# A second tile for ScalarE's tap products in a 31-tap convolution

## The chip, the cores and the metric

The kernel runs on one core of one Trainium2 chip. The metric is device time in microseconds (us) for one execution. Five instruction streams of the core matter here: TensorE (PE, with its weight loads PEld), VectorE (DVE), ScalarE (ACT), GpSimd (POOL) and SyncE (SP, which issues most DMAs). Each of them takes its instructions strictly in the order in which they stand in its stream.

## The reference

One decoder layer over 2048 tokens of width 1024: a modulated RMSNorm, one input projection whose columns feed three mixers (a gated recurrence "HGRN", a sparse attention with an indexer and top-k, and a convolution module), an output projection, and an MLP of width 4096. The change concerns the convolution module only:

```python
def conv_module(u, cv_w, cv_b, ln_w, ln_b):
    a, b = jnp.split(u, 2, axis=-1)
    h = a * jax.nn.sigmoid(b)
    h = lax.conv_general_dilated(h, cv_w[:, None, :], ...,   # causal, one filter of 31 taps
        feature_group_count=CV_WIDTH) + cv_b                 # for each of 256 channels
    ... LayerNorm over channels, then silu
```

## The kernel before

The sequence is worked in four blocks of 512 tokens. For each block `in_block` runs the input projection as a row of units: each unit is one column block of the weights, multiplied with the block's activations on PE (`mm_T`, line 427, 24 products of 128x128 by 128x512 each, or `n_part`, line 1293, for the units whose result is wanted by token). The first block splits its weights into a high and a low part on the way (ACT line 320, then POOL line 321); later blocks reload what was split. Each unit's result is evicted from PSUM by ACT and DVE (`ev_...` functions).

Everything else is written as generators in queues ("fast" for HGRN, "conv" for the convolution, "idx", "tk" and "at" for the attention, "ada" for modulation vectors) which `step` and `half` advance between the units. That sets the order in which instructions are emitted. A scheduler then orders each engine's stream by its own simulated timeline of the whole program, so a change in the waits of one step can move others.

The convolution of a block lies with channels on partitions and tokens along the row, in two halves of 128 channels (`m` = 0, 1). The units `cb` and `ca` make the gated input: `ev_cb` writes the sigmoid into a tile with the tag `csg0` or `csg1` (line 573), `ev_ca` multiplies it into `hc` (line 579), after which the `csg` tile is free until the half's sum `cacc` is written to the same tag (line 605). `conv_gen` then works a half's 31 taps. Tap 0 and the even taps are a chain on DVE that accumulates in PSUM (`cx`, lines 588 and 600). The odd taps are products on ACT (tap 1 into `cside`, line 594, the other 14 into `ctap`, line 597), which POOL adds to `cside` one after the other (line 598). Line 605 on DVE joins both. `CB = 1`, so there is one `ctap` tile: ACT's next product has to wait until POOL has read the last one. `cx` and `cside` have one buffer as well, so the second half starts after line 605 of the first.

Two other chains share these engines in the same stretch of time. HGRN (`hgrn_gen`) goes through seven levels, each with small products on PE (lines 684, 709, 717) and updates of `q` and `k` on DVE (lines 674, 675, after lines 681 and 692). The top-k search runs passes on DVE (line 931) and ends in a branch (lines 945 to 948, with the exact search that is rarely taken behind it).

Of the kernel before, what the change touches and what calls it, by code (L numbers as in the profile page):

```python
# [8 lines left out]
F32 = mybir.dt.float32  # L9
# [11 lines left out]
P = 128  # L21
D = 1024
L = 2048
TB = 512
# [38 lines left out]
CT = 2  # L63
# [4 lines left out]
CB = 1  # L68
# [10 lines left out]
def trunk(ctx, tc, x, c, ada_w, ada_b, norm_mix_w, norm_mlp_w, w_in, hg_lb_logits,  # L79
# [22 lines left out]
    def nm(s):  # L102
        uid[0] += 1
        return f"{s}_{uid[0]}"

    def dma(o, i):
        return nc.sync.dma_start(o, i)
# [10 lines left out]
    def ps_cx():  # L118
        return px["p"].tile([P, 512], F32, tag="cx", bufs=1, name=nm("cx"))
# [9 lines left out]
    def ps_xp(i):  # L129
        return {'0': ps_ax, '1': ps_mm, '2': ps_at, '3': ps_po}[XP[i]]()  # L130
# [58 lines left out]
    def col(key, i=0, n=1):  # L189
        return cols[:, offs[key] + i:offs[key] + i + n]  # L190
# [62 lines left out]
    def rpow(dst, src, w, scale):  # L253
        G.tensor_scalar(dst, src, scale, EPS, op0=OP.mult, op1=OP.add)
        G.tensor_tensor(dst, dst, nhalf.to_broadcast([P, w]), OP.pow)
# [189 lines left out]
    hp = S1.enter_context(tc.tile_pool(name="hgrn", bufs=1))  # L445
# [9 lines left out]
    def st(tag, bufs, w=TB, dt=F32, shape=None):  # L455
        return hp.tile(shape or [P, w], dt, tag=tag, bufs=bufs, name=nm(tag))
# [126 lines left out]
    def conv_gen(b):  # L583
        accs = []
        for m in range(2):
            hc = conv[m]
            acc = ps_cx()
            V.tensor_scalar(acc, hc[:, 0:TB], cvc[:, m, 0:1], col("cvb", m), op0=OP.mult, op1=OP.add)
            side = None
            for w in range(1, TAPS):  # L590
                if w % CT == 1:
                    if side is None:
                        side = hp.tile([P, TB], F32, tag="cside", bufs=1, name=nm("cside"))
                        A.mul(side, hc[:, w:w + TB], cvc[:, m, w:w + 1])
                    else:
                        tap = hp.tile([P, TB], F32, tag="ctap", bufs=CB, name=nm("ctap"))
                        A.mul(tap, hc[:, w:w + TB], cvc[:, m, w:w + 1])  # L597
                        G.tensor_tensor(side, side, tap, OP.add)  # L598
                else:
                    V.scalar_tensor_tensor(acc, hc[:, w:w + TB], cvc[:, m, w:w + 1], acc,  # L600
                                           op0=OP.mult, op1=OP.add)
                if w % 3 == 0:
                    yield 1300
            total = hp.tile([P, TB], F32, tag=f"csg{m}", bufs=1, name=nm("cacc"))
            V.tensor_tensor(total, acc, side, OP.add)
            accs.append(total)
        yield 1200
        tot = st("cside", 1)
        G.tensor_tensor(tot, accs[0], accs[1], OP.add)
        pm = ps_xp(4)  # L610
        T.matmul(pm, o256.to_broadcast([P, P]), tot, start=True, stop=True)
        for m in range(2):
            V.tensor_tensor(accs[m], accs[m], pm, OP.subtract)
        sqs = []
        for m in range(2):
            sq = st("cu", 2)
            A.activation(sq, accs[m], AF.Square)
            sqs.append(sq)
        G.tensor_tensor(sqs[0], sqs[0], sqs[1], OP.add)
        yield 1500  # L620
        pv = ps_xp(5)
        for t in range(4):
            T.matmul(pv[:, t:t + 1], sqs[0][:, t * P:(t + 1) * P], ones[:, 0:1], start=True, stop=True)
        rc = hp.tile([P, 4], F32, tag="crs", bufs=1, name=nm("crs"))
        V.tensor_copy(rc, pv[:, :4])
        rpow(rc, rc, 4, 1.0 / 256.0)
        yield 1500
        rs = ps_xp(6)
        for t in range(4):
            T.matmul(rs[:, t * P:(t + 1) * P], rc[:, t:t + 1].to_broadcast([P, P]), ident, start=True, stop=True)  # L630
        for m in range(2):
            V.scalar_tensor_tensor(accs[m], accs[m], col("lnw", m), rs, op0=OP.mult, op1=OP.mult)
            sg = st("cu", 2)
            A.activation(sg, accs[m], AF.Sigmoid, bias=col("lnb", m))
            o = st("cu", 2)
            V.scalar_tensor_tensor(o, accs[m], col("lnb", m), sg, op0=OP.add, op1=OP.mult)
            dma(mx_d[b][6 + m], o)
        yield 3000
# [491 lines left out]
    def in_block(b, xts, nxt):  # L1130
        act = first_units(xts) if b == 0 else to_act(xts, a1, sh1, half if TM else None)
        for u, (pieces, ev, m) in enumerate(in_units):
# [38 lines left out]
            if ev is ev_ca and m == 1:  # L1171
                queues["conv"].append(conv_gen(b))
# [94 lines left out]
    for b in range(NB):  # L1267
        for what, g, f in mlp_order(b):
            if what == "out":
                specs += kept_specs("out", out_specs())  # L1270
            elif what == "strassen":
                for kind, g_, i in strassen_order(b):
                    if kind == "m1":
                        specs += kept_specs((kind, g_, i), None)
                    else:
                        w = PRODUCTS[i][1]
# [403 lines left out]
```

## Time and profile before

| | us |
|---|---|
| median of 3 runs | 2960.59 (2958.34 to 2962.74) |
| the profiled execution | 2951.88 |
| its span (first to last instruction) | 2950.1 |
| PE busy | 2794.7 (95%) |
| DVE busy | 1681.9 (57%) |
| ACT busy | 1297.8 (44%) |
| POOL busy | 1239.4 (42%) |

The busy times are sums over the span; stages differ. The convolution's instructions lie between 118 and 946 us, one group for each of the four blocks. Idle time of an engine costs only where another engine, in the end PE, waits for it.

### The profile page before, as it was taken

The numbers are of one execution on the slowest core, as the hardware profiler recorded it, in microseconds if no ns is written. First come the engines' busy times: TensorE is split into PE (matmuls) and PEld (weight loads), VectorE is DVE, ScalarE is ACT, GpSimd is POOL, SyncE is SP. The second block draws the span as 40 slices with busy tenths as digits, with TensorE's granted clock in tenths as the row PEclk, the third lists the DMA queues.
The fourth block names the chain that finished last, engine by engine and source line by source line (L and its number), as shares of the span: only waits on it lengthen the run. The fifth ranks groups of instructions, "written<-read, shape, count | busy, mean of one in ns | idle before, by whom it ended". The sixth has DMA issues, their size and how long they took to land. (4 is left out here: it accounts for less than half of the span.)

```text
span 2950.1 us, 42864 instructions
## 1 busy us (share of the span) xinstructions
PE 2794.7 (95%) x14116; PEld 2313.0 (78%) x14116; DVE 1681.9 (57%) x3450; ACT 1297.8 (44%) x2706; POOL 1239.4 (42%) x1163
## 2 busy tenths in 40 slices
PE   6999989899999989999998999999999999999997
PEld 5888878778788867788786888877788888777776
DVE  7684586966536354847849637385853221254455
ACT  4445464545324235556545544444553333243333
POOL 7573251225214255567656322224432223335444
PEclk9999999899999999999999999999999999999999
DMA  8977666566655567899978867677686767686666
GB/s 284 291 250 238 207 209 216 187 202 196 212 188 170 189 227 247 268 288 307 297 244 271 283 206 225 202 217 253 229 285 207 233 204 232 212 276 222 227 228 208
DMA packets 428075, 688.62 MB, mean 233 GB/s; under 512 B 43383, under 2 KB 171452, under 8 KB 427836
## 3 DMA queue, kind: packets, MB, share of 16 engines
q1 hardware_dynamic: 427680, 685.67, 72.2%
q8 instruction: 113, 1.85, 0.3%
q14 instruction: 126, 1.03, 0.1%
q10 hardware_dynamic: 156, 0.07, 0.0%
HBM read 532.74 MB, written 152.84 MB: 232 GB/s over the span
## 5 line engine op out<-in xcount | busy, mean ns | idle before, releaser
L427 PE MATMUL mm<-ah,wk 128*128 128x512 f32 x1920 | 518.9, 402 | 5.2 <-DVE adrow L780 2.5
L427 PEld LDWEIGHTS mm<-ah,wk 128*128 128x128 f32 x1920 | 359.6, 192 | 80.1 <-DVE adrow L780 3.1
L321 POOL TENSOR_TENSOR wlo<-wraw,whi 128x512 fp32r<-128x512 f32 x210 | 287.7, 1390 | 204.2 <-ACT whi L320 142.5
L1011 POOL TENSOR_TENSOR pT<-L,pT 128x512 fp32r<-128x512 f32 (+3 forms) x160 | 194.1, 1214 | 309.8 <-ACT pT L1010 194.0
L829 DVE SCALAR_TENSOR_TENSOR s<-r,iw_s,s 128x512 f32<-128x512 f32 (+3 forms) x266 | 242.3, 911 | 113.4 <-ACT r L824 104.3
L427 PE MATMUL mm<-al,wk 128*128 128x512 f32 x960 | 262.9, 396 | 0.0
L981 DVE CUSTOM_DVE_ANT_0 L<-at,bias 128x512 f32<-128x512 f32 (+3 forms) x152 | 93.4, 618 | 223.8 <-PE at L979 183.8
L427 PEld LDWEIGHTS mm<-al,wk 128*128 128x128 f32 x960 | 179.9, 190 | 36.2
L1317 PE MATMUL mm<-wk,hh 128*128 128x512 f32 x640 | 199.5, 400 | 2.6 <-DVE acc L1570 2.0
L824 ACT ACTIVATE r<-ix 128x512 f32<-128x512 f32 (+3 forms) x256 | 133.5, 554 | 154.3 <-PE ix L822 107.2
L273 POOL TENSOR_TENSOR hl<-hr,hh 128x512 fp32r<-128x512 f32 x96 | 128.0, 1334 | 172.6 <-ACT hh L265 149.1
L598 POOL TENSOR_TENSOR cside<-cside,ctap 128x512 f32<-128x512 f32 x112 | 149.5, 1335 | 110.4 <-ACT ctap L597 102.6
L320 ACT CAST whi<-wraw 128x512 fp32r<-128x512 f32 x210 | 121.5, 619 | 152.8 <-DMA wraw<-in_mlp_w_dram 37.3
L427 PE MATMUL ax<-ah,wk 128*128 128x512 f32 x720 | 186.4, 393 | 1.1 <-DMA wk<-wk_d 1.1
L931 DVE TENSOR_SCALAR_CACHE_REDUCE cum<-s,ssm 128x384 bf16<-128x384 f32 (+13 forms) x112 | 165.4, 1477 | 7.9 <-POOL s L833 5.7
L427 PEld LDWEIGHTS ax<-ah,wk 128*128 128x128 f32 x720 | 134.4, 188 | 31.1 <-ACT hc L1451 1.5
L1009 ACT COPY L<-at 128x512 f32<-128x512 f32 (+3 forms) x160 | 82.8, 521 | 171.1 <-PE at L1001 169.3
L1477 PE MATMUL mm<-wk,hc 128*128 128x512 f32 x588 | 148.1, 397 | 3.9 <-DVE acc L1485 3.7
L995 ACT ACTIVATE L<-L,nmx 128x512 f32<-128x512 f32 (+3 forms) x160 | 103.7, 650 | 100.4 <-DVE nmx L990 100.0
L1317 PEld LDWEIGHTS mm<-wk,hh 128*128 128x128 f32 x640 | 118.1, 189 | 28.7 <-DVE acc L1570 2.4
L1477 PEld LDWEIGHTS mm<-wk,hc 128*128 128x128 f32 x588 | 109.6, 188 | 33.8 <-DVE acc L1485 7.5
L1317 PE MATMUL ax<-wk,hh 128*128 128x512 f32 x384 | 123.4, 400 | 0.6 <-DVE acc L1570 0.3
(368 smaller groups left out, 6338.5 us busy)
## 6 DMA issues: line engine op xcount, KB each, us to landing
wk<-wk_d SPq DMA_DIRECT2D x776, 256.0 KB, 4.4
wk<-wk_d SPq DMA_DIRECT2D x196, 512.0 KB, 5.1
wk_d<-whi SPq DMA_DIRECT2D x210, 256.0 KB, 3.5
wk_d<-wlo SPq DMA_DIRECT2D x210, 256.0 KB, 5.5
wraw<-in_mlp_w_dram SPq DMA_DIRECT2D x68, 512.0 KB, 5.8
kc<-sk_d SPq DMA_DIRECT2D x112, 256.0 KB, 3.0
vc<-v_d SPq DMA_DIRECT2D x112, 256.0 KB, 4.3
adw<-in_ada_w_dram SPq DMA_DIRECT2D x128, 128.0 KB, 3.4
```

What stands on the lines that cost most here:

```text
L273: e.tensor_tensor(lo[:, i:j], src[:, i:j], hi[:, i:j].bitcast(F32), OP.subtract)
L320: A.copy(hi, src)
L321: G.tensor_tensor(lo, src, hi.bitcast(F32), OP.subtract)
L427: T.matmul(ps, ww[k], aa[k], start=(n == 0 and k0 == 0), stop=(n == len(order) - 1 and k1 == NK))
L598: G.tensor_tensor(side, side, tap, OP.add)
L824: A.activation(r[:, :w], ps[:, :w], AF.Relu, scale=32.0 ** -0.5)
L829: V.scalar_tensor_tensor(s[:, c0:c0 + w], r[:, :w], iw, s[:, c0:c0 + w], op0=OP.mult, op1=OP.add)
L931: V.tensor_scalar(dump, s, t, -AIM - i * STEP, op0=OP.is_ge, op1=OP.add, accum_out=d)
L995: A.activation(lt[:, :w], lt[:, :w], AF.Exp, bias=nmx, accum_out=sm[:, cb:cb + 1])
L1011: G.tensor_tensor(pT[:, :nt, 1], lv, pT[:, :nt, 0].bitcast(F32), OP.subtract)
L1317: T.matmul(ps, aa[f][:, tok * P:(tok + 1) * P], ww[i], start=(first and n == 0), stop=(last and n == 5))
L1477: T.matmul(bank[t], aa[:, k, t * P:(t + 1) * P], ww[k], start=(i in (0, 2, 4) and n == 0), stop=(n == 5), skip_group_check=True)
```

## The change

The 14 products that follow the first one now alternate between two tiles: the old `ctap` tile, and the tile of the tag `csg1`, which held the second half's gate. Both have one buffer. Tap 3 goes to `csg1`, tap 5 to `ctap`, and so on.

```diff
                     else:
-                        tap = hp.tile([P, TB], F32, tag="ctap", bufs=CB, name=nm("ctap"))
+                        tap = hp.tile([P, TB], F32, tag=("ctap", "csg1")[w // CT % 2], bufs=1, name=nm("ctap"))
                         A.mul(tap, hc[:, w:w + TB], cvc[:, m, w:w + 1])
                         G.tensor_tensor(side, side, tap, OP.add)
```

Number and kind of the instructions stay the same on every engine. Their order changes, since the scheduler places them anew: within the four convolution stretches on all engines, and at a few places of the MLP. Three places follow.

POOL, first block, the start of the second half (`cside_1956` is this half's sum, `wlo` the low parts of weights). Before:

```order
L598 TENSOR_TENSOR cside_1956<-cside_1956,ctap_1959 128x512
L598 TENSOR_TENSOR cside_1956<-cside_1956,ctap_2026 128x512
L321 TENSOR_TENSOR wlo_2043<-wraw_1962,whi_2042 128x512
L321 TENSOR_TENSOR wlo_2047<-wraw_1962,whi_2046 128x512
L598 TENSOR_TENSOR cside_1956<-cside_1956,ctap_2030 128x512
L598 TENSOR_TENSOR cside_1956<-cside_1956,ctap_2034 128x512
L321 TENSOR_TENSOR wlo_2136<-wraw_2040,whi_2135 128x512
L321 TENSOR_TENSOR wlo_2140<-wraw_2040,whi_2139 128x512
```

and in the changed kernel:

```order
L598 TENSOR_TENSOR cside_1956<-cside_1956,ctap_1959 128x512
L948 UNCONDITIONAL_BRANCH
L598 TENSOR_TENSOR cside_1956<-cside_1956,ctap_2026 128x512
L598 TENSOR_TENSOR cside_1956<-cside_1956,ctap_2030 128x512
L254 TENSOR_SCALAR hrs_1436<-hrs_1436 128x4
L321 TENSOR_TENSOR wlo_1965<-wraw_1883,whi_1964 128x512
L255 TENSOR_TENSOR hrs_1436<-hrs_1436,nhalf 128x4
L598 TENSOR_TENSOR cside_1956<-cside_1956,ctap_2034 128x512
L321 TENSOR_TENSOR wlo_1969<-wraw_1883,whi_1968 128x512
L598 TENSOR_TENSOR cside_1956<-cside_1956,ctap_2116 128x512
L321 TENSOR_TENSOR wlo_2043<-wraw_1962,whi_2042 128x512
L321 TENSOR_TENSOR wlo_2047<-wraw_1962,whi_2046 128x512
```

Five adds of the second half stand before `wlo_2043` where there were two, and the half begins a unit earlier.

DVE, first block, the joining add of the first half (`cacc_1952`), with the eviction `slo` of projection units around it. Before, it stands behind the top-k branch, among the first steps after it:

```order
L900 MATCH_REPLACE s_747<-top_2038,s_747 128x384
L932 TENSOR_SCALAR ssm_2227<-ssm_2227 128x1
L939 TENSOR_SCALAR ssm_2227<-ssm_2227 128x1
L605 TENSOR_TENSOR cacc_1952<-cx_1350,cside_1352 128x512
L902 TENSOR_SCALAR bias_995<-s_747 128x384
L940 TENSOR_SCALAR ssm_2227<-ssm_2227 128x1
L543 SCALAR_TENSOR_TENSOR slo_1928<-mm_1893,shi_1927 128x512
L588 TENSOR_SCALAR cx_1954<-hc_1334,cvc,cols 128x512
```

and in the changed kernel, ahead of the branch (which follows `L946`):

```order
L742 SCALAR_TENSOR_TENSOR sa_1398<-sa_1398,fb_1094,ax_1393 128x128 x2
L750 SCALAR_TENSOR_TENSOR S_st_194<-sa_1398,fb_1094,ax_1393 128x128
L605 TENSOR_TENSOR cacc_1952<-cx_1350,cside_1352 128x512
L588 TENSOR_SCALAR cx_1954<-hc_1334,cvc,cols 128x512
L540 TENSOR_TENSOR slo_1719<-mm_1684,shi_1718 128x512
L945 CAST far_1756<-at_1754 1x1
L600 SCALAR_TENSOR_TENSOR cx_1954<-hc_1334,cvc,cx_1954 128x512
L946 TENSOR_LOAD far_1756
```

The joining add now comes right behind `L750`, and `slo_1719` and the branch stand behind it. The four steps of the second half's chain (`L600`) that follow the branch stand ahead of `slo_1928`.

PE, first block, the first level of the second HGRN head (`q_1510`), among the products of a unit of line 1293. Before:

```order
L1293 MATMUL mm_2143<-whi_2139,al_538 128x256
L1293 MATMUL mm_2143<-wlo_2136,ah_504 128x256
L1293 MATMUL mm_2143<-wlo_2136,ah_515 128x256
L709 MATMUL ax_1653<-q_1510,k_1417 128x64 x4
L1293 MATMUL mm_2143<-wlo_2140,ah_526 128x256
```

and in the changed kernel:

```order
L1293 MATMUL mm_2236<-wlo_2047,ah_355 128x256
L1293 MATMUL mm_2236<-wlo_2047,ah_366 128x256
L1293 MATMUL mm_2236<-whi_2042,ah_333 128x256
L1293 MATMUL mm_2236<-whi_2042,ah_344 128x256
L709 MATMUL ax_1653<-q_1510,k_1417 128x64 x4
```

It stands 28 products of line 1293 later. On DVE, the update of `q_1510` (line 674) that it waits for stands later too: ahead of it have come seven steps of line 600, one each of lines 656, 681 and 937 and two of line 725 (on 128x64 and 128x32 elements), and one pass of line 931 on 128x384 elements has gone behind. The last rows ahead of that update are, before:

```order
L688 TENSOR_TENSOR at_1576<-ax_1579,ident 128x256
L692 TENSOR_TENSOR q_1510<-q_1510,f_1414 128x4x128
L675 TENSOR_TENSOR k_1417<-k_1417,f_1414 128x256
L600 SCALAR_TENSOR_TENSOR cx_1954<-hc_1334,cvc,cx_1954 128x512
L932 TENSOR_SCALAR ssm_2227<-ssm_2227 128x1
L936 TENSOR_SCALAR ssm_2227<-ssm_2227 128x1
L725 TENSOR_TENSOR fb_2438<-fb_2438 128x128
L690 COPY_PREDICATED at_1576<-lmask,ax_1579 128x128
L674 TENSOR_TENSOR q_1510<-q_1510,f_1414 128x4x64
```

and in the changed kernel:

```order
L656 SCALAR_TENSOR_TENSOR q_2084<-mm_2050,u_2085 128x4x128
L688 TENSOR_TENSOR at_1576<-ax_1579,ident 128x256
L692 TENSOR_TENSOR q_1510<-q_1510,f_1414 128x4x128
L675 TENSOR_TENSOR k_1417<-k_1417,f_1414 128x256
L600 SCALAR_TENSOR_TENSOR cx_1954<-hc_1334,cvc,cx_1954 128x512
L937 RECIPROCAL ssm_2227<-ssm_2227 128x1
L725 TENSOR_TENSOR fb_2438<-fb_2438 128x32
L681 TENSOR_TENSOR q_2084<-q_2084,f_2006 128x4x64
L690 COPY_PREDICATED at_1576<-lmask,ax_1579 128x128
L674 TENSOR_TENSOR q_1510<-q_1510,f_1414 128x4x64
```

Work of the next head (`q_2084`) now stands ahead of this update. In the second and third block the HGRN products move later in PE's stream in the same way, by up to some 46 of the units' products, and are back in their old places by the blocks' ends.

## The prediction

> **What bounds the kernel now.** I read the page's totals first, then the table of windows over the four stretches in which the convolution runs, then the rows of the tap tile, then PE's gaps in those stretches, and last DVE's and POOL's rows around the joining add.
>
> ```profile
> span 2950.1 us, 42864 instructions
> PE 2794.7 (95%) x14116; PEld 2313.0 (78%) x14116; DVE 1681.9 (57%) x3450; ACT 1297.8 (44%) x2706; POOL 1239.4 (42%) x1163
> ```
>
> PE is busy for 95% of the span: 2950.1 - 2794.7 = 155.4 us is all that better waiting could give. The chain of waits is listed for the end of the program alone, so the table of windows must speak for the convolution. It has each stretch and some time after it (length, PE, PE's loads, DVE, ACT, POOL, granted PE clock, DMA):
>
> ```profile
> core 0: us, PE busy (x) PEld busy (x) DVE busy (x) ACT busy (x) POOL busy (x), PEclk, DMA share, GB/s
> 118.00:218.00 100.00, 93.82 (x533) 79.88 (x532) 91.31 (x222) 53.20 (x102) 78.65 (x64) 0.98 0.80 249
> 218.00:250.00 32.00, 31.06 (x193) 27.29 (x192) 11.67 (x39) 18.78 (x44) 11.94 (x12) 1.00 0.93 282
> 355.00:445.00 90.00, 78.96 (x424) 64.77 (x424) 76.73 (x142) 51.40 (x98) 47.42 (x47) 0.94 0.65 205
> 650.00:725.00 75.00, 67.45 (x366) 55.53 (x366) 58.20 (x125) 48.89 (x95) 42.51 (x39) 0.93 0.61 193
> 900.00:946.00 46.00, 44.06 (x251) 38.12 (x250) 32.72 (x55) 21.73 (x43) 27.17 (x22) 1.00 0.56 175
> ```
>
> PE's idle time in the stretches is 6.2 + 11.0 + 7.6 + 1.9 = 26.7 us. In the first, DVE is busy for 91% and POOL for 79%; ACT is at little over half in all. So the engine next to PE here is DVE, and neither ACT nor POOL. The tap tile:
>
> ```profile
> L597 ACT ACTIVATE ctap<-hc,cvc x112: 706/724/769, 120.0 to 942.1; 128x512 f32<-128x512 f32 x112
> L598 POOL TENSOR_TENSOR cside<-cside,ctap x112: 1260/1290/2182, 120.8 to 942.9; 128x512 f32<-128x512 f32 x112
> who waited for it (us, times):
>   POOL cside L598: 102.6, 84
>   ACT ctap L597: 85.4, 68
>   DVE cacc L605: 1.5, 1
> ```
>
> ACT waits 85.4 us for POOL to free the tile, and POOL 102.6 us for the next product. Outside this pair the only wait is 1.5 us of DVE, once in eight joining adds. PE is not in the list. What PE does wait for in the stretches:
>
> ```profile
> 174.93 2.11 PE L427 MATMUL mm<-ah,whi 128*128 128x512 f32 x8 [1.11 <-DVE slo L543]
> 184.07 0.64 PE L1293 MATMUL mm<-whi,ah 128*128 128x256 f32 x4
> 184.55 0.64 PE L1293 MATMUL mm<-whi,al 128*128 128x256 f32 x4
> 189.37 1.54 PE L709 MATMUL ax<-q,k 128*128 128x64 f32 x8 [3.42 <-DVE q L674]
> ...
> 364.54 0.49 PE L749 MATMUL ax<-sa,q 128*128 128x128 f32 x2 [1.92 <-DVE sa L742]
> 398.65 1.08 PE L709 MATMUL ax<-q,k 128*128 128x64 f32 x8 [1.75 <-DVE k L675]
> 421.79 0.81 PE L717 MATMUL ax<-q,k 128*32 128x32 f32 x16 [2.32 <-DVE k L675]
> 697.30 1.10 PE L709 MATMUL ax<-q,k 128*128 128x64 f32 x8 [2.35 <-DVE k L675]
> ```
>
> All of it is DVE: evictions and HGRN steps. The change takes nothing off DVE; through the order it only decides when DVE gets to them.
>
> **The tap loop itself.** 112 products and 112 adds stay. What goes is the alternation, product 0.72 us, add 1.29 us, neither beside the other. With two tiles the product runs beside the add before it, and a tap costs POOL's 1.29 us alone. The most that can come off the side chain is POOL's 102.6 us, 12.8 us for each of eight halves. None of it is on PE's path, so I cost it at nothing. Its cover is PE's main products, which do not read the convolution's result inside the stretch; the result is wanted by the output projection, long after. If the cover were gone, the side chain's price is the 1.5 us that DVE waited. ACT's instructions behind a waiting product (evictions, weight casts) come free earlier as well, but no row above shows PE held by ACT. What is late next in a half is DVE with its own 15 taps, and then the joining add in DVE's order.
>
> The new tile also brings a wait: the first half's tap 3 cannot be written before `hc` of the second half has read the gate there (line 579). In the order, ACT therefore issues tap 5 ahead of tap 3, and POOL starts adding after the second `halo` copy. Behind the waiting product on ACT stands the next `r` eviction of the indexer. The scheduler has put two weight casts ahead of it, so I take no cost. The bounds are 0 and a tap or two of POOL's time, 2.6 us, by which the first half would end later; that is regained within the half, since POOL waited there for taps.
>
> **Block 1, DVE's order.** Here the change has its clearest effect on PE. The rows that price it:
>
> ```profile
> L600 DVE SCALAR_TENSOR_TENSOR cx<-hc,cvc,cx 128x512 f32<-128x512 f32 x30 | 22.3, 745 | 0.0
> ...
> 189.87 0.67 DVE L656 SCALAR_TENSOR_TENSOR q<-mm,u 128x512 f32<-128x512 f32 x1
> 190.46 0.21 DVE L725 TENSOR_TENSOR fb<-fb 128x64 f32<-128x64 f32 x1
> 191.43 0.41 DVE L681 TENSOR_TENSOR q<-q,f 128x256 f32<-128x256 f32 x1
> 154.82 0.61 DVE L931 TENSOR_SCALAR_CACHE_REDUCE cum<-s,ssm 128x384 bf16<-128x384 f32 x1
> ```
>
> Ahead of the `q` update that PE waited 3.42 us for at 189.37 now stand seven more steps of line 600 (7 x 0.745 = 5.2 us), one each of lines 656 and 681 (0.67 + 0.41), two small ones of line 725 (some 0.4) and one of 937 (under 0.2), and one pass of line 931 fewer (0.61): 5.2 + 1.1 + 0.6 - 0.6 = 6.3 us. PE's product stands 28 products of line 1293 later, which at 0.48 us for four (184.07 to 184.55) is 3.4 us. DVE was busy for 91 of these 100 us and 6.31 of the others are the branch's (below), so there is no slack to take it up, and the difference falls on PE: +2.9 us. The bounds are -3.4 (DVE turns out to have the slack, and the old wait is covered) and +6.3.
>
> The joining add of the first half stands ahead of the top-k branch now:
>
> ```profile
> 161.35 0.35 DVE L750 SCALAR_TENSOR_TENSOR S_st<-sa,fb,ax 128x128 f32<-128x128 f32 x1
> 169.88 0.63 DVE L890 SCALAR_TENSOR_TENSOR s<-cum,s 128x384 f32<-128x384 bf16 x1 [6.31 <-DVEq L948]
> 173.14 0.68 DVE L605 TENSOR_TENSOR cacc<-cx,cside 128x512 f32<-128x512 f32 x1
> 166.16 1.29 POOL L598 TENSOR_TENSOR cside<-cside,ctap 128x512 f32<-128x512 f32 x1
> 944.18 0.69 DVE L605 TENSOR_TENSOR cacc<-cx,cside 128x512 f32<-128x512 f32 x1 [1.54 <-POOL cside L598]
> ```
>
> DVE came past `L750` at 161.70. POOL's last add of that half ended at 167.45 in the old loop. If nothing were gained, DVE would now wait 5.75 us; if the alternation gives more than that, nothing. Half of the most is 12.8 / 2 = 6.4 us, so near zero is likely, but the start is later too; I take 1.5 us, the one wait of this kind that the trace has. Behind it on DVE stand `slo_1719`, the branch with its 6.31 us of fetch, and `slo_1928`, which PE already waited 1.11 us for, so it reaches PE whole. Four more steps of line 600 ahead of `slo_1928` make that wait longer, but they are among the seven counted. Block 1: +2.9 + 1.5 = +4.4 us.
>
> **Blocks 2 to 4.** Both shifts recur: conv steps come earlier on DVE, HGRN products later on PE. In the second block they are between 5 and 10 us on either side and in the third DVE moves less than PE, so some of the old waits shrink. The four waits shown at 364 to 697 us (1.92 + 1.75 + 2.32 + 2.35 = 8.3 us) are the bound of the gain. The bound of the loss is 1.54 us at each of the other six joining adds, 9.2 us. Between them I take -3 us, a third of the way to the gain, as PE's rows moved at least as far as DVE's. The few changed places in the MLP I take at nothing: the kernel's late PE rows wait little, and the same products stand there.
>
> **A rule against it.** In the first stretch DVE's two-input step of line 675 reads, and in the time after it:
>
> ```profile
> L675 DVE TENSOR_TENSOR k<-k,fb x9: 405/1508/1518, 122.7 to 216.7; 128x256 f32<-128x256 f32 x9
> L675 DVE TENSOR_TENSOR k<-k,fb x14: 403/416/1508, 216.7 to 345.4; 128x256 f32<-128x256 f32 x14
> ```
>
> The same step has a median of 1.51 us where POOL is busy for 79% and 0.42 us after it. By rows I add nothing, since the adds that lengthen it stay 112 and only lie closer together. The Trainium skill ("SBUF — State Buffer", section "Who interferes with whom") says that a DVE instruction with two SBUF inputs and a GpSimd instruction that reads SBUF exclude each other for a whole instruction. The trace agrees so far. By that rule a denser POOL costs DVE more inside the stretch: with POOL's 78.7 us in some 90 us, 87% in place of 79%, one more of the 18 steps of lines 674 and 675 there would take the extra 1.1 us, and the sum would be +2.5 us in place of +1.4.
>
> **The sum.** +4.4 - 3.0 = +1.4 us on the profiled execution of 2951.9 us (its span and 1.8 us around it). That execution was 8.7 us below the median of the runs, 2960.6, so I carry the difference over: 2962.0 us. What a measurement can tell from no change here is 0.2%, 5.9 us, and the forecast is no change.
>
> **Rivals.** *HGRN's waits are covered (faster).* With its products later in PE's stream, the waits of blocks 1 to 3 vanish: 3.4 + 8.3 = 11.7 us, 2949 us. For it: every one of them is PE arriving first, and PE's rows moved later in three blocks. The granted clock of 0.94 and 0.93 in two stretches, against 1.00 after one and in the last, could come back as well; at full clock throughout, 0.06 x 90 + 0.07 x 75 = 10.7 us more at the very most. Against: DVE's steps moved later with them. It decides when DVE has 6 us of slack per head; in block 1 it had none.
>
> *The joining adds wait (slower).* With its own steps moved forward, DVE meets line 605 before POOL is done, in all eight halves, with evictions and HGRN behind it. At the 1.54 us of the one row that is 8 x 1.54 = 12.3 us, 2973 us. For it: they moved forward on DVE, one even past a branch. Against: POOL's chain is the one that gets shorter, and seven of eight did not wait. From 0.75 us each it is more than 5.9 us.
>
> *The second tile isn't used (no change).* If the gate's lifetime kept ACT waiting, ACT and POOL would still alternate at 2.1 us a tap, and the time would stay at 2960.6. Only the first tap of a half meets the gate, so I give it little.
>
> **How the numbers follow.** Forecast, with everything within 5.9 us: 0.44; the unused tile, the same result: 0.04. Covered HGRN waits, in part or whole: 0.25. Waiting joining adds: 0.27. So faster 0.25, same 0.48, slower 0.27. The forecast's own range is 2956 to 2967. For 8 in 10 it reaches to the covered waits' 2949 and a little past the waiting adds' 2973, to 2975.
>
> **What would show it.** Right: POOL's wait for ACT at line 598 falls from 102.6 us to under 40; each half's adds take under 1.6 us a tap where no weight part stands between them; the convolution's last instruction of block 1 comes some 10 us earlier than 218; PE's idle time in the four stretches stays at 22 to 33 us; in block 1 PE waits 5 to 12 us in all for `slo` of line 543 and for the first product of line 709 (4.5 us before). Wrong: POOL's wait unchanged (the tile), PE idle in the stretches under 20 us (covered waits), or DVE rows of line 605 with waits of over 6 us in total.

## The result and the profile after

| | before | changed |
|---|---|---|
| median of the timed runs | 2959.47 us (2957.27 to 2962.74) | 2977.88 us (2974.85 to 2980.91) |
| ratio | | 1.007, 95% interval 1.005 to 1.009 |
| the profiled execution | 2951.88 us | 2974.85 us |
| mean granted clock of TensorE in it, as a share of 2.4 GHz | 0.979 | 0.976 |

The change makes the kernel 0.7% slower, 18 us; the forecast was 2962.0 us and no change. A second set of runs (e8 below) gave 1.0055 (1.0035 to 1.0074). The totals of the profile after:

```profile
span 2973.1 us, 42960 instructions
PE 2804.8 (94%) x14116; PEld 2318.9 (78%) x14116; DVE 1688.6 (57%) x3450; ACT 1296.2 (44%) x2706; POOL 1233.1 (41%) x1163
```

The span grew by 23.0 us. PE is busy for 10.1 us more with the same 14116 products, and idle for 168.3 us in place of 155.4, 12.9 us more. The first part goes with the granted clock, by this estimate: (1 - 0.979) x 2950.1 = 62.0 us were lost to it before, (1 - 0.976) x 2973.1 = 71.4 us after. The five counts of instructions are those of before, but the count of all of them is not: 42960 where it was 42864. The additional ones are steps that only wait for or set a semaphore, most of them POOL's at line 598 (85 in place of 1, 17 ns each). The experiment e14 below has such steps too, 102 of them, and shows no loss.

The table of windows, cut at the same products of PE's main stream in both kernels, tells where the 23.0 us went. Columns as before: length, PE, PE's loads, DVE, ACT, POOL, granted clock, DMA. First the kernel before:

```profile
0.00:104.40 104.40, 75.20 (x380) 64.07 (x381) 66.75 (x124) 44.96 (x77) 68.20 (x68) 0.97 0.93 299
104.40:230.00 125.60, 118.48 (x692) 101.93 (x691) 104.97 (x262) 63.94 (x127) 92.17 (x75) 0.99 0.83 254
230.00:608.00 378.00, 347.85 (x2036) 297.79 (x2034) 261.36 (x690) 196.14 (x432) 116.30 (x143) 0.95 0.66 211
608.00:980.30 372.30, 352.05 (x2066) 301.64 (x2065) 206.13 (x429) 142.71 (x311) 119.99 (x113) 0.96 0.59 190
980.30:2950.10 1969.80, 1901.08 (x8952) 1547.54 (x8950) 1042.66 (x1949) 850.10 (x1761) 842.70 (x765) 0.99 0.75 241
```

and the changed one:

```profile
0.00:106.20 106.20, 76.55 (x379) 64.68 (x380) 67.14 (x124) 44.89 (x77) 67.55 (x68) 0.95 0.93 293
106.20:235.10 128.90, 118.84 (x678) 101.49 (x677) 108.37 (x256) 62.95 (x123) 87.70 (x73) 0.96 0.79 247
235.10:621.40 386.30, 355.21 (x2051) 301.44 (x2050) 268.72 (x695) 197.07 (x437) 118.19 (x146) 0.93 0.66 207
621.40:999.80 378.40, 352.59 (x2066) 301.43 (x2065) 205.62 (x429) 142.57 (x310) 119.51 (x112) 0.97 0.58 186
999.80:2973.10 1973.30, 1901.57 (x8952) 1549.84 (x8950) 1038.77 (x1949) 848.73 (x1761) 840.14 (x765) 0.99 0.75 241
```

The first convolution stretch lost 3.3 us, the second and the stage behind it 8.3, the third and fourth 6.1; the start and the MLP lost 1.8 and 3.5, where the order is nearly the same and one execution against another says little. In the second stretch 7.4 of the 8.3 us are PE being busy for longer. Some 2 us of that are 15 small products that were moved over from the first stretch (x2051 in place of x2036, and x678 in place of x692 there), so the first lost more by as much; the rest goes with a granted clock of 0.93 in place of 0.95. In the third and fourth 5.6 of the 6.1 us are idle time.

The tap tile does what the change says (line 598's row, then how long its engines stood idle before its instructions, until what: us and times):

```profile
L598 POOL TENSOR_TENSOR cside<-cside,ctap x112: 1261/1296/1792, 128.9 to 947.4; 128x512 f32<-128x512 f32 x112
...
  POOL cside L598: 45.3, 52
  ACT ctap L597: 27.3, 14
  DVE hc L579: 13.1, 4
```

POOL's wait for the next product fell from 102.6 to 27.3 us, and DVE is no longer among those that waited for the tile. Block 1's convolution ends at POOL's line 609, 209.58 us (next fence), where it was 218.9. PE's larger waits in that block:

```profile
209.58 1.29 POOL L609 TENSOR_TENSOR cside<-cacc,cacc 128x512 f32<-128x512 f32 x1 [2.89 <-DVE cacc L605]
...
150.18 2.69 PE L427 MATMUL mm<-ah,whi 128*128 128x512 f32 x8 [2.23 <-DVE q L656]
...
183.84 2.50 PE L427 MATMUL mm<-ah,whi 128*128 128x512 f32 x5 [4.70 <-DVE slo L543]
...
200.72 1.00 PE L709 MATMUL ax<-q,k 128*128 128x64 f32 x8
...
207.46 1.07 PE L709 MATMUL ax<-q,k 128*128 128x64 f32 x8 [2.09 <-DVE k L675]
```

The first product of `q_1510`, for which PE waited 3.42 us before, is the row at 200.72: it stands behind 62 products of line 1293 where there were 34, 28 more as in the order shown above, and PE does not wait for it at all. The row at 207.46 is the next level's product, which had no wait before.

The wait for the eviction `slo` of line 543 was 1.11 us and is 4.70. DVE's rows ahead of that eviction:

```profile
176.09 0.56 DVE L890 SCALAR_TENSOR_TENSOR s<-cum,s 128x384 f32<-128x384 bf16 x1 [4.67 <-DVEq L948]
...
176.63 0.75 DVE L600 SCALAR_TENSOR_TENSOR cx<-hc,cvc,cx 128x512 f32<-128x512 f32 x1
...
178.28 0.74 DVE L600 SCALAR_TENSOR_TENSOR cx<-hc,cvc,cx 128x512 f32<-128x512 f32 x1
...
180.01 0.74 DVE L600 SCALAR_TENSOR_TENSOR cx<-hc,cvc,cx 128x512 f32<-128x512 f32 x1
...
181.50 0.74 DVE L600 SCALAR_TENSOR_TENSOR cx<-hc,cvc,cx 128x512 f32<-128x512 f32 x1
...
183.11 0.68 DVE L543 SCALAR_TENSOR_TENSOR slo<-mm,shi 128x512 fp32r<-128x512 f32 x1
```

Four of the convolution's steps, 3.0 us, stand between the branch and the eviction. That is the order. (Beside it, the step of line 902 just ahead of `slo` took 1.03 us where it had taken 0.35.)

The wait at 207.46 shows the other thing. DVE's rows ahead of it, and POOL's add beside the first of them:

```profile
202.95 1.28 DVE L725 TENSOR_TENSOR fb<-fb 128x4 f32<-128x4 f32 x1
...
205.90 1.08 DVE L674 TENSOR_TENSOR q<-q,fb 128x256 f32<-128x256 f32 x1
...
202.92 1.30 POOL L598 TENSOR_TENSOR cside<-cside,ctap 128x512 f32<-128x512 f32 x1
```

DVE's small update and POOL's add begin almost together and end together, at 204.23 and 204.22 us. The same update took 0.15 us before (at 196.51, with no add beside it), the one before it (128x8 elements, 1.25 us) 0.15 as well, and the step of line 674 took 0.45: 2.9 us more on DVE, and PE waits 2.09.

Block 4 shows the same at length. Before, DVE's small updates `fb` of line 725 and what follows, with POOL's adds beside them (DVE first, then POOL):

```profile
911.03 0.17 DVE L725 TENSOR_TENSOR fb<-fb 128x16 f32<-128x16 f32 x1
...
912.56 0.15 DVE L725 TENSOR_TENSOR fb<-fb 128x4 f32<-128x4 f32 x1
...
908.61 1.27 POOL L598 TENSOR_TENSOR cside<-cside,ctap 128x512 f32<-128x512 f32 x1 [0.83 <-ACT ctap L597]
...
912.64 1.29 POOL L598 TENSOR_TENSOR cside<-cside,ctap 128x512 f32<-128x512 f32 x1 [0.29 <-ACT cside L594]
```

and the same in the changed kernel, with PE's wait that follows:

```profile
931.96 0.77 DVE L725 TENSOR_TENSOR fb<-fb 128x16 f32<-128x16 f32 x1
932.65 0.74 DVE L600 SCALAR_TENSOR_TENSOR cx<-hc,cvc,cx 128x512 f32<-128x512 f32 x1
933.31 0.76 DVE L725 TENSOR_TENSOR fb<-fb 128x8 f32<-128x8 f32 x1
...
934.65 0.76 DVE L725 TENSOR_TENSOR fb<-fb 128x4 f32<-128x4 f32 x1
...
935.99 0.74 DVE L764 SCALAR_TENSOR_TENSOR r<-ax,cols,gate 128x512 f32<-128x512 f32 x1
...
928.66 8.07 POOL L598 TENSOR_TENSOR cside<-cside,ctap 128x512 f32<-128x512 f32 x6
...
936.79 1.65 PE L684 MATMUL ax<-q,k 128*128 128x192 f32 x4 [3.37 <-DVE r L764]
```

Before, the updates ran between two adds, after 909.88 and up to 912.64, and one of 128x4 elements took 0.15 us. In the changed kernel six adds run without a pause (8.07 us), and it takes 0.76 us. The steps of line 725 end at 932.73, 934.07 and 935.41 us, 1.34 us apart, and the six adds take 1.345 us each: each such step, both of whose inputs lie in SBUF, now ends with an add. The steps of line 600 between them, which accumulate in PSUM, keep their 0.74 us. Behind this row of steps stands `r` of line 764, for which PE waits 3.37 us.

So there were two suspects: the new order, and the adds that lie closer together.

### The profile page after: what moved, and what is told of

The parts are those of the page before. It is cut to its first block, busy times and chain, and to the rows that moved or that the text cites. A ratio compares the mean times of both kernels' runs of the same rounds, so it can differ in the third digit from the quotient of the medians.

```text
span 2973.1 us, 42960 instructions
## 1 busy us (share of the span) xinstructions
PE 2804.8 (94%) x14116; PEld 2318.9 (78%) x14116; DVE 1688.6 (57%) x3450; ACT 1296.2 (44%) x2706; POOL 1233.1 (41%) x1163
## 4 chain that ended last, share of the span: by engine, by line
PE 45%; DVE 4%; DMA 3%; POOL 1%; issue 1%; ACT 1%; SPq 0%; POOLq 0%; DVEq 0%; ACTq 0%
PE mm L1317 11%; PE mm L427 11%; PE ax L427 8%; PE ax L1317 6%; PE mm L1477 4%; PE po L1013 2%; PE at L979 1%; PE at L1001 1%; PE ix L822 1%; DMA wk<-wk_d 1%; PE at L1317 1%; DVE cum L931 1%; DMA tr<-in_mlp_w_dram 1%; DVE s L829 1%; POOL wk L379 1%
## 5 line engine op out<-in xcount | busy, mean ns | idle before, releaser
L1011 POOL TENSOR_TENSOR pT<-L,pT 128x512 fp32r<-128x512 f32 (+3 forms) x160 | 189.8, 1188 | 352.1 <-ACT pT L1010 214.8
L598 POOL TENSOR_TENSOR cside<-cside,ctap 128x512 f32<-128x512 f32 x112 | 151.1, 1349 | 41.2 <-ACT ctap L597 27.3
L995 ACT ACTIVATE L<-L,nmx 128x512 f32<-128x512 f32 (+3 forms) x160 | 103.8, 650 | 102.6 <-DVE nmx L990 102.4
```

Of the source, the lines that this page charges most:

```text
L995: A.activation(lt[:, :w], lt[:, :w], AF.Exp, bias=nmx, accum_out=sm[:, cb:cb + 1])
L1011: G.tensor_tensor(pT[:, :nt, 1], lv, pT[:, :nt, 0].bitcast(F32), OP.subtract)
```

## The experiments

All ratios are to the kernel before, timed beside it on the same chip. Where a kernel is "held to an order", a function at the end of the program adds edges of issue order between an engine's neighbouring instructions. They bring no semaphore: e10, the kernel before held to its own order with shorter adds, has 42863 instructions in its profile where the kernel before has 42864. The kernel before itself was not timed under these edges.

```diff
     with tile.TileContext(nc, schedule_with_timeline_sim=True) as tc:
         trunk(tc, *args, o)
+        pin(tc, ORDERS)      # for each engine: tc.add_manual_dep(this, the one before it, NoSync)
```

**e1: two tiles, old order.** The changed kernel, with

```diff
+ORDERS = [old order of DVE, PE, SP, POOL, and of ACT without line 597]
```

> The changed kernel (two tap tiles), with every engine held to the order it had before the change; only ScalarE's 112 tap products are left free. Theory A (the loss comes from the new order, not from the tile): ratio to the kernel before 0.998 to 1.002. Theory B (with two tiles GpSimd's adds lie denser and lengthen VectorE's two-input steps, whatever the order): ratio 1.003 to 1.007, VectorE busy some 1688 us in place of 1682. By both GpSimd's wait for the tap products falls under 60 us from 102.6, but not to the 27.3 of the changed kernel, as the adds keep their old places.

Measured: 1.0031 (1.0019 to 1.0043). Theory A in its pure form falls: with the old order there is still a loss. Theory B is not confirmed by it: POOL's wait for the products fell to 45.6 us, as both theories had it, but DVE is busy for 1681.1 us and not for some 1688, and the largest new wait of PE is for another engine:

```profile
378.94 0.80 PE L1013 MATMUL po<-pT,vc 128*128 128x256 f32 x2 [5.01 <-POOL pT L1011]
```

In block 2 POOL stood 7.61 us behind an add whose tap had to wait for the gate, with `pT` of the attention behind it. So a part of e1's loss is the gate's.

**e2: one tile, new order.** The kernel before, with

```diff
+ORDERS = [new order of DVE, PE, SP, POOL, and of ACT without line 597]
```

> The kernel before (one tap tile), with every engine held to the order of the changed kernel; ScalarE's 112 tap products are left free. Theory A (order): ratio 1.004 to 1.010, as in the changed kernel or worse, since the joining adds now stand early on VectorE and GpSimd's chain is as slow as before: waits of VectorE at the joining adds of 5 us or more in all. Theory B (denser adds): 0.998 to 1.002.

Measured: 1.0192 (1.0179 to 1.0205). The new order needs the second tile and costs 1.9% without it. (In its profile, taken at a mean granted clock of 0.653, DVE waited at all eight joining adds.)

**e3: one tile, another order.**

```diff
-HA, HE, HF, HC = 0, 0, 0, 0
+HA, HE, HF, HC = 0, 0, 0, 100
```

> The kernel before with one tap tile; the convolution's steps get a slightly higher priority in the scheduler (offset 100), which re-orders about as many rows as the change did (on TensorE 3574 rows stand at another place, 3386 in the changed kernel). Theory C (the order before was an unusually good one, and any other costs the like): ratio 1.003 to 1.010. Theory A in its narrow form (what costs is that the convolution's steps on VectorE come earlier because the tap products do): 0.998 to 1.003.

Measured: 1.0016 (1.0004 to 1.0029). A small loss: less than theory C had, and not nothing.

**e4: two tiles, VectorE's old order only.** The changed kernel, with

```diff
+ORDERS = [old order of DVE]
```

> The changed kernel (two tap tiles) with VectorE alone held to the order it had before; the other engines are ordered anew around that. If VectorE's order carries the loss: ratio 0.998 to 1.003. If the order of TensorE or the DMA queue carries it: 1.004 to 1.008.

Measured: 1.0089 (1.0076 to 1.0102). An old order for one engine among new ones for the others is no better. DVE's order alone does not carry the loss.

**e5: two tiles, old order, ScalarE too.** The changed kernel, with

```diff
+ORDERS = [old order of DVE, PE, SP, POOL, and of ACT without tap 3 of the first halves]
```

> As e1, but ScalarE's tap products are held to their old places too, but for tap 3 of the first half in each block, which has to wait for the gate. So the second tile is all that is left of the change. Theory D (the loss of e1 came from ScalarE taking the tap products ahead of evictions that others wait for): ratio to the kernel before 0.998 to 1.001. Theory B (the second tile lets GpSimd's adds come closer together, and that delays VectorE at the places where TensorE waits for it): 1.002 to 1.004, as in e1.

Measured: 1.0041 (1.0027 to 1.0055). Theory D falls: it was not ScalarE's products going ahead. But in this order POOL stood waiting for tap 3 until the second half's gate had been read, once in each block:

```profile
126.81 3.17 POOL L598 TENSOR_TENSOR cside<-cside,ctap 128x512 f32<-128x512 f32 x2 [6.76 <-ACT ctap L597]
```

so closer adds and the wait for the gate were not yet told apart.

**e6 and e7: two tiles in one block alone.**

```diff
-tag=("ctap", "csg1")[w // CT % 2]
+tag=("ctap", "csg1")[w // CT % 2 if b == 0 else 0]     # e6; b == 1 in e7
```

> Two tap tiles in the first block alone, the order chosen by the scheduler: in the first block it is that of the changed kernel, in the later blocks that of the kernel before. If the step for block 1 of the prediction was right and the later blocks carry the rest: ratio 1.001 to 1.003 (4.4 us of waits, and what the granted clock adds). If block 1 carries all of it: 1.005 to 1.007.

> Two tap tiles in the second block alone, the order chosen by the scheduler: the first block is as before, the second as in the changed kernel, the third and fourth differ from both. If blocks 2 to 4 gain, as the prediction had it: ratio 0.998 to 1.000. If they lose: 1.002 to 1.005.

Measured: e6 1.0027 (1.0012 to 1.0042), e7 1.0059 (1.0042 to 1.0077). Block 1's tile costs 8 us, with 4.4 inside the interval. The second block's tile, which the prediction had as a gain, comes with a loss too; as e7 has yet another order in its third and fourth block, how much of it is block 2's is not shown. The two add up to more than the whole.

**e8: the changed kernel again.**

> The changed kernel once more, on the same chip as e5 to e7, to have its ratio and the mean of its granted clock over more runs: 1.006 to 1.009. If the clock carries half of the loss, the mean granted clock is 0.973 to 0.976 where the kernel before has 0.979 to 0.981; if it is waits alone, the two are the same to 0.001.

Measured: 1.0055 (1.0035 to 1.0074); mean granted clock 0.977 over its seven runs, 0.979 over the nineteen of the kernel before. (1 - clock) x span, the estimate from above, is 67.9 us on average, and 61.8 before: 6 of the 17 us. The clock's share is a third here and less than half, smaller than expected, and the ratio lies just under the range expected.

**e9: one tile, POOL kept busy.**

```diff
                         G.tensor_tensor(side, side, tap, OP.add)
+                        fill = hp.tile([P, 256], BF16, tag="cfill", bufs=1, name=nm("cfill"))
+                        G.tensor_tensor(fill, side[:, :256], side[:, 256:], OP.add)
```

> The kernel before, one tap tile, every engine held to its old order, with one more instruction on GpSimd behind each of the 112 adds: a sum of the two halves of the side row into a spare tile (256 columns, nobody reads it), which fills the time in which GpSimd waited for the next product. ScalarE runs no further ahead than before. Theory B (GpSimd's denser work delays VectorE's steps with two inputs in SBUF, and TensorE with them): ratio 1.002 to 1.008, and in block 1 13 to 17 of VectorE's HGRN steps of lines 674, 675, 681, 692, 725 and 648 lengthened by over 0.5 us, where the kernel before has 11 and the changed kernel 16. Theory E (ScalarE running ahead, or the tile itself): 0.998 to 1.0015, and 11 such steps.

Measured: 1.0059 (1.0037 to 1.0081), and 22 lengthened HGRN steps in block 1 where the kernel before has 11. One tile, the old order, ScalarE no freer than before, and a loss like the changed kernel's is there: theory E is not needed for it. (The filler takes some 0.74 us and adds 86.8 us to POOL's busy time; it is more work as well as less pause. It also holds ScalarE, which waits 110.4 us for the tap tile in place of 85.4, and a part of the loss may come that way.)

**e10 and e11: short adds, in the old order with one tile and in the new order with two.**

```diff
-G.tensor_tensor(side, side, tap, OP.add)
+G.tensor_tensor(side[:, :64], side[:, :64], tap[:, :64], OP.add)
```

> The kernel before, one tap tile, every engine held to its old order; GpSimd's 112 adds work on 64 of the 512 columns, so seven eighths of the odd taps' sum is left out. Theory B: TensorE's waits for VectorE in block 1 shrink, under 8 lengthened HGRN steps there in place of 11, ratio 0.992 to 0.998. Theory E: the adds are off TensorE's path, 0.998 to 1.001.

> The changed kernel, two tap tiles, every engine held to its new order, with the same short adds as e10. If all of the change's loss comes over GpSimd's adds: the ratio is within 0.0015 of that of e10. If the new order costs by itself: it is 0.003 or more above that of e10.

Measured: e10 0.9922 (0.9899 to 0.9946), e11 0.9964 (0.9948 to 0.9980). Long adds cost 0.8% already in the kernel before, though no row of PE's waits names line 598, and in e10 block 1 has 4 lengthened HGRN steps. (e10 also frees ScalarE, which waits 24.5 us for the tile in place of 85.4. That this is not what the second tile does is shown by e12 below, where ScalarE waits 16.9 us and the kernel is slower.) With the adds nearly gone, the new order is still 0.9964 / 0.9922 = 1.0042 of the old one, some 0.003 to either side by the two intervals: it has a price of its own.

**e12 and e13: the half's own gate as the second tile.**

```diff
-tag=("ctap", "csg1")[w // CT % 2]
+tag=("ctap", f"csg{m}")[w // CT % 2]
```

That gate has been read before the half's taps begin, so nothing waits for it. e12 is held to the old order, row by row; e13 is left to the scheduler.

> Two tap tiles, the second one now the tile of the half's own gate (csg0 for the first half, csg1 for the second), which has been read before the half's taps begin, so no product waits for a gate. Every engine, ScalarE too, is held to the old order, row by row. Theory F (e5 lost by the wait for the second half's gate, 6.8 to 8.5 us of GpSimd's queue in each block): ratio to the kernel before 0.998 to 1.001. Theory B (closer adds delay VectorE): 1.002 to 1.005, as e5. By both the wait of GpSimd at its second add of each block, 6.8 to 8.5 us in e5, is gone.

> The same two tiles as e12, with the order left to the scheduler, as in the changed kernel. If the order that the scheduler makes for two tiles loses by itself (e11 against e10: 0.4%): ratio 1.002 to 1.006. If the changed kernel's loss came from the gate, in the order and in the wait: 0.998 to 1.001.

Measured: e12 1.0031 (1.0016 to 1.0045), e13 1.0076 (1.0055 to 1.0098). Theory F falls as the main cause: without any wait for a gate, and with every instruction in its old place, the second tile alone costs 0.3%. POOL's adds do lie closer: it waited 41 times for a product in e12, 84 times before. With the scheduler's own order it is the changed kernel's loss again, 1.0045 of e12.

**e14: e12 with short adds.**

> As e12 (two tiles, the second one that of the half's own gate, every engine held to the old order), with GpSimd's adds on 64 of 512 columns, so seven eighths of the odd taps' sum is left out. Theory B (the second tile loses because the adds lie closer): the ratio is that of e10, 0.992, to 0.0015. If ScalarE's freedom is what loses: 0.003 above, 0.995 or more.

Measured: 0.9920 (0.9904 to 0.9935), the same as e10 with one tile, within some 0.003 by the two intervals. So no cost of the second tile is seen where the adds are short, and 0.3% where they are long: it loses over the adds. The difference is only just clear of the noise.

How this reaches PE is best read at the three places of block 1 where PE waits for DVE, since these kernels have the same order. In the kernel before they are the 1.11 and 3.42 us that the prediction shows, and

```profile
147.06 2.11 PE L427 MATMUL mm<-ah,whi 128*128 128x512 f32 x8 [1.05 <-DVE q L656]
```

PE's rows with waits in e12:

```profile
148.31 2.11 PE L427 MATMUL mm<-ah,whi 128*128 128x512 f32 x8 [1.11 <-DVE q L656]
...
176.51 2.11 PE L427 MATMUL mm<-ah,whi 128*128 128x512 f32 x8 [1.41 <-DVE slo L543]
...
191.50 1.94 PE L709 MATMUL ax<-q,k 128*128 128x64 f32 x8 [4.29 <-DVE q L674]
```

in e9 (where line numbers are one to three higher):

```profile
151.05 2.11 PE L428 MATMUL mm<-ah,whi 128*128 128x512 f32 x8 [1.20 <-DVE q L659]
...
182.52 3.07 PE L428 MATMUL mm<-ah,whi 128*128 128x512 f32 x8 [3.70 <-DVE slo L544]
...
199.13 1.94 PE L712 MATMUL ax<-q,k 128*128 128x64 f32 x8 [4.52 <-DVE q L677]
```

and all that is left in e10 between 140 and 215 us:

```profile
185.18 1.08 PE L709 MATMUL ax<-q,k 128*128 128x64 f32 x8 [1.95 <-DVE q L674]
```

The sum of the three is 5.6 us before, 6.8 in e12, 9.4 in e9 and 2.0 in e10 (3.7 in e14, whose profiled execution is its longest). In e9 the way from POOL to PE can be followed at `slo`. DVE's steps between the branch and that eviction:

```profile
174.97 1.65 DVE L893 SCALAR_TENSOR_TENSOR s<-cum,s 128x384 f32<-128x384 bf16 x1 [4.64 <-DVEq L951]
...
177.14 0.82 DVE L901 TENSOR_SCALAR sm<-i,sm 128x8 f32<-128x8 f32 x1
...
178.19 1.01 DVE L902 TENSOR_TENSOR top<-top,sm 128x8 f32<-128x8 f32 x1
```

They took 0.63, 0.21 and 0.15 us before (there lines 890, 898, 899): 2.5 us more on DVE, and PE waits 2.6 us more.

The groups of DVE's step of line 675 from 104 to 980 us (count, busy, mean ns) go the same way in these kernels; the kernel before and e9 (there line 678):

```profile
L675 DVE TENSOR_TENSOR k<-k,fb 128x256 f32<-128x256 f32 x79 | 45.5, 576 | 0.0
```
```profile
L678 DVE TENSOR_TENSOR k<-k,fb 128x256 f32<-128x256 f32 x78 | 53.7, 688 | 0.0
```

In e10 the same step has 460 ns, in e14 464, in e12 620. In the changed kernel, with its other order, it has 552, less than before; there the steps of line 725 are the ones that grew. e12's profiled execution, 2951.8 us, is one of the shortest of its twelve runs, so its rows show the places and not the whole of the 0.3%: its convolution part (105.6 to 985.1 us) is 3.6 us longer than before, with DVE busy for 4.9 us more, and its MLP, where nothing was changed, 4.8 us shorter.

**e15 and e16: one tile, two more orders.** `HC = -100` and `HC = 400` in the line of e3.

> The kernel before with one tap tile; the convolution's steps get a lower priority in the scheduler (offset -100): from the first block's end on, products and HGRN steps move to earlier places, the convolution's to later ones. Theory C (any order of this size of change costs 0.2 to 0.4%): ratio 1.002 to 1.005. If it matters which way the convolution moves: 0.995 to 1.000 here.

> The kernel before with one tap tile; the convolution's steps get a higher priority (offset 400, where e3 had 100), so they come earlier. Theory C: ratio 1.002 to 1.005. If it matters which way the convolution moves: more than e3's 1.0016, 1.003 to 1.010.

Measured: e15 1.0034 (1.0020 to 1.0047), e16 1.0174 (1.0158 to 1.0190), at mean granted clocks of 0.974 and 0.973. All three other orders are slower than the one before, the convolution moved later or earlier. Theory C holds in a weaker form: the 0.4% of the new order is nothing peculiar to this change; e3 and e15 cost 0.2 and 0.3%, and the convolution moved far ahead costs 1.7%, more than was expected of e16 by either view.

**e17 and e18: whole taps moved from POOL to DVE.** `CT = 3` and `CT = 4` in place of 2.

> The kernel before with one tap tile and CT = 3: every third tap goes to ScalarE and GpSimd in place of every second, so 72 adds in place of 112, and 40 more of VectorE's steps of line 600 (40 x 0.745 = 29.8 us on VectorE). The scheduler orders it anew. If the adds' delay outweighs VectorE's own work and the new order: ratio 0.994 to 0.999. If VectorE, busy for 91% of the first stretch, is the limit: 1.003 to 1.012.

> The same with CT = 4: 8 taps of a half and so 56 adds in all on GpSimd, 56 more steps of line 600 (41.7 us) on VectorE. If the adds' delay outweighs: 0.990 to 0.998. If VectorE is the limit: 1.005 to 1.015, more than e17.

Measured: e17 1.0048 (1.0029 to 1.0067), e18 1.0007 (0.9992 to 1.0022). Neither beats the kernel before. The one with more work on DVE is not the slower one, so DVE as the limit is not what decides; these two also have new orders, and what each part costs was not taken apart. No version in this study that adds all the taps beats the kernel before.

## Why the prediction was wrong

**The loss has two parts, and each was forecast near nothing.** The second tile by itself costs 0.3% (e12), over the adds (e14); the new order costs 0.4% by itself (e11 against e10 and e14, e13 against e12). Together that is 0.7%, as in the first measurement, 1.007. That they add up so simply is not shown: on the one chip that ran both, the changed kernel is only 1.0014 of the same two tiles in the old order (e8 against e5, some 0.0024 to either side).

**The step that failed first: "The tap loop itself ... I cost it at nothing."** It looked for the tap tile among the waits, found PE nowhere in that list, and called PE's main products the cover. The way to PE was not a wait: POOL's add makes DVE's instruction longer, which no row counts as idle, and PE then waits for that DVE step. The working even had the rows, line 675 at 1.51 us beside POOL's adds and at 0.42 after them, and then added nothing "since the adds that lengthen it stay 112 and only lie closer together". That is the mistake: DVE's steps ran short in the pauses between adds, 0.83 us and more, and the pauses were what the second tile took away. The rule weighed there, of the Trainium skill ("SBUF — State Buffer", section "Who interferes with whom"), pointed the right way, and e9, e10 and e14 agree with it. Its price in the prediction, one step of 1.1 us, was too small by far against the 9 us of e12's 0.31%. (How those 9 us are made up is not shown row by row: e12's own profile has 3.6 us of them.)

**The second step that failed: blocks 2 to 4, "-3 us".** From the second stretch to the fourth the changed kernel lost 8.3 + 6.1 = 14.4 us, some 2 of them by the products moved over from the first. The choice there, a third of the way towards the gain since PE's rows moved as far as DVE's, had no duration behind it. That PE's products stand later helps only if DVE's steps keep their length, and in block 4 they did not (0.15 to 0.76 us, then a wait of 3.37).

**The third: the granted clock had no term.** It was priced as a possible gain of a rival and not as a cost of more waits. By the profiled executions it is 9.4 of the 23.0 us, by the runs of e8 6 of 17. Some 2 of the 9.4 us lie in the first 106 us, ahead of the convolution, and in the third and fourth stretch the clock was higher than before (0.97, 0.96) while PE idled more, so the 6 of 17 is the better figure, and the clock did not follow PE's waits everywhere.

**Near in number by luck: block 1.** +4.4 us of waits were forecast, the stretch is 3.3 us longer, and PE idles in it for 2.9 us more (7.1 to 10.1). But the parts are others. The sum put +2.9 us at the first product of `q_1510`; there the old wait of 3.42 us is gone, the lower bound of that step, so "there is no slack to take it up" was wrong at this place. The joining add's 1.5 us did not come. In their stead PE waits 3.6 us more for `slo` (1.11 to 4.70), behind the four steps of line 600 that the working had counted for `q_1510`, 1.2 us more for `q` of line 656 (1.05 to 2.23), and 2.09 us at the next product of line 709, behind lengthened steps. The waits for `slo` and for the first product of line 709 sum to 4.7 us, just under the 5 to 12 that were given as a sign of being right.

**Right in kind, no cost: the tile's own waits.** POOL's wait for products is 27.3 us (under 40 forecast), block 1's convolution ends 9.3 us earlier (some 10), ACT waited 13.1 us in all for the gate. No DVE wait at line 605 is left.

**The rivals.** Waiting joining adds: not in the changed kernel; with one tile in the new order, e2, they appear, and there the loss is 1.9%. Covered HGRN waits: the idle time did not fall. One of them was covered (`q_1510`), and others came. In the four stretches the idle time is 33.2 us, by the sum of their windows in the changed kernel, just over the 22 to 33 given, and 26.7 before:

```profile
sum 321.00, PE 287.77 PEld 238.65 DVE 262.53 ACT 173.37 POOL 199.90; mean PE 71.94 PEld 59.66 DVE 65.63 ACT 43.34 POOL 49.97
```

The unused tile fell with the first row. What the tile cost, longer DVE steps under denser adds, was in the text as a rule worth 1.1 us and in no rival.

**What stays open.** Which of the many moved rows make up the order's 0.4% was not settled: e4, e6 and e7 show that neither one engine's order nor one block's can be put back without making a third order. The wait for the gate (e5 against e12: 1.0041 and 1.0031, intervals that overlap) may cost 0.1% or nothing. Whether lengthened DVE steps make up all of the second tile's 0.3% is open too: that it comes over the adds is shown, and single waits of PE were followed back to such steps, but not their sum.

## What to carry to other kernels

Before a second buffer is given to a pair of engines that is off the critical path, ask who else used the pauses that the buffer takes away: here they were VectorE's chance to run steps with both inputs in SBUF, and shortening the "idle" pair's wait by 75 us made the kernel slower. Look for this in the spread of durations (min, median, max of one step on one shape), since a lengthened step is in no list of waits. Where a scheduler re-orders a tuned program, count the new order as a cost by itself, and price it by running another order with nothing else changed.

## What the runs showed of the hardware

- A VectorE step with both inputs in SBUF waited for the end of the GpSimd add that was running, whatever its own size: 128x4 elements took 0.15 us between two adds, 0.76 beside adds without a pause, and 1.28 where it began 0.03 us behind an add. (Which of the two goes first is not settled by so short a lead: in the kernel before a step of 128x8 elements, at 195.12 us, 0.03 us behind an add, took 0.15, and the add 1.35 us in place of 1.29.) VectorE's 3450 steps are busy for 38.6 us less in all when the adds are cut to 64 columns (e10), and for 18.4 us more with the filler (e9), by these rows of e10 and e9 against the 1681.9 us before:

```profile
PE 2789.4 (95%) x14116; PEld 2309.3 (79%) x14116; DVE 1643.3 (56%) x3450; ACT 1297.0 (44%) x2706; POOL 1127.9 (38%) x1163
```
```profile
PE 2806.1 (95%) x14116; PEld 2321.7 (78%) x14116; DVE 1700.3 (57%) x3450; ACT 1297.8 (44%) x2706; POOL 1326.2 (45%) x1275
```

- VectorE's steps that accumulate in PSUM with one input in SBUF (line 600) were not touched: 0.74 us between the same adds.
- Slower kernels also had a lower mean granted clock: 0.980 with short adds (e10), 0.979 before, 0.977 changed (e8), 0.973 in e16. In block 1 it can be seen at single waits. In the kernel before the clock was 0.50, the lower of its two levels (1.2 GHz in place of 2.4), from 189.8 to 193.2 us, right behind PE's wait of 3.42 us, and four products of line 1293 took 1.05 us there in place of 0.64. In the changed kernel it was 0.50 from 151.5 to 154.9 us, behind the wait of 2.23 us, and from 182.2 to 189.0 us, at the wait of 4.70, and 1.00 behind the wait of 2.09. So three of these four waits were paid for twice.
